# A hybrid attention and SSD layer: the SSD half of the output projection computed by seven products ahead of attention

## The chip, the cores and the metric

The kernel runs on one core of one Trainium2 chip. The metric is device microseconds of one launch, as the median of several runs; lower is better.

## The reference, cut to what matters

One layer, with one sequence of 2048 tokens, a model width of 1024 and float32 everywhere. An input projection feeds two branches of width 1024, attention and an SSD scan. Both are gated and normed, laid side by side and multiplied by one 2048 x 1024 matrix; a residual and a LayerNorm follow.

```python
proj = einsum('bsd,de->bse', x, w_in)                    # 1024 -> 6672 columns
q, k, v, z_att, z_ssm, xbc, dt_raw = split(proj)
y_att = wts[0] * o1 + wts[1] * o2 + wts[2] * o3          # windowed attention, dilations 1, 4, 16
y_att = rms_norm(y_att * silu(z_att), att_norm_g)
...
y = ssd_chunked(xs, dt, a, bm, cm) + d_skip * xs         # chunks of 128 tokens
y_ssm = rms_norm(y * silu(z_ssm), ssm_norm_g)
mix = concatenate([y_att, y_ssm], axis=-1)               # (2048, 2048)
x = layer_norm((2 * DEPTH) ** 0.25 * x + mix @ w_out, ln_g, ln_b)
```

`rms_norm(u, g)` is u / sqrt(mean(u^2) + eps) * g. The factor per token can therefore be applied after the matrix product, and g can be folded into the rows of `w_out`.

## The kernel before, in words

Every float32 product is made of three TensorE (PE) products of split numbers: each operand is a high part (a cast) and a low part (the operand minus its high part), and high x high, high x low and low x high are added in PSUM. A split so costs a cast on ScalarE (ACT) and a subtraction on VectorE (DVE) or GpSimd (POOL).

The kernel has four stretches. Between them and inside them PE, DVE, ACT and POOL run in the order in which the program is written; the order of SyncE's DMAs (SP) is set by a scheduler.

1. The v columns of the projection, with the sums that the second stretch needs.
2. The rest of the input projection, as 44 jobs. A job makes a 256 x 1024 tile of the transposed projection from 2 x 2 blocks by the Strassen-Winograd scheme, which needs seven products in place of eight. A product is 12 matmuls of 128x512 (four slices of the inner dimension, three each), so a job has 84. The token side (`token_side`, seven operands B11, T1, B21, T2, B22, T4, T3, each a high and a low tile of 1 MB) stays for a phase of jobs and is loaded anew where the phase changes, on POOL's queue: phase 0 has 10 jobs, phase 1 has 22, phase 2 has 12. The column side (`column_side`) is built for each job from a raw 256-column piece: ACT casts, POOL subtracts, DVE forms the sums. `products` writes a job; after each of its seven products `flush` adds one to a count, and `after(n, f)` and `later` hang other work on later counts. In this way the 32 SSD units (16 chunks of tokens times 2 groups of channels) run between the products from count 161 on: `spots` says at which count a unit begins, and `ssd1` to `ssd6` are its steps, one a count. `d_us` receives the gated SSD output, and `ssd6` writes a split copy of the first four blocks of 128 tokens to `d_uh`. `wout_load` and `split_w` scale the SSD rows of `w_out` by the norm's gain, split them and store them to `d_wo`, hung on counts 35 to 55.
3. Attention, in 8 pairs of heads. What a pair still needs after its last tile (`statistics`, `gather`, `weights`, `combine`) is a chain of DMAs through DRAM with DVE work between them, written into the program of the next pair. The combined output goes to `d_ua`, and that of pair 7 stays in SBUF (`u7`, tiles named PT). During pair 7 the weights of the SSD half are loaded (`load_w`).
4. The output projection with the norms, for 16 blocks of 128 tokens. Each block has two products of 48 matmuls, `(n, 1)` for the SSD half and `(n, 0)` for the attention half, in the order of `order`: the SSD halves of blocks 0 to 3 first, then their attention halves, and from block 4 on the two halves in turn. The loads of the attention half's weights from `d_wo` are written behind the second product. A half needs `split` (its DVE copy of pair 7 at L994, ACT's cast at L995, the subtraction at L996), `squares` (ACT at L1000, the DVE reduction at L1002), `product` (L1025 to L1027, and at L1031 the matmul that adds up the squares over channels) and `add` (reciprocal at L1039, scaling and adding at L1043). `norm` closes a block: L1049 to L1063 on DVE, then two POOL multiplications and additions with the LayerNorm's vectors (L1064, L1065) and the store.

## Time and profile before

| | |
|---|---|
| median of 3 runs | 2184.16 us (2184.16 to 2184.79) |
| profiled execution, its own time | 2171.41 us |
| span in its profile | 2169.6 us |
| mean clock granted to PE | 0.972 |
| PE busy | 2048.0 us, 94% |
| weight loads (PEld) busy | 1703.7 us, 79% |
| DVE busy | 1394.1 us, 64% |
| ACT busy | 1154.4 us, 53% |
| POOL busy | 1092.5 us, 50% |
| moved by DMA | 525.26 MB, mean 242 GB/s |

The profile is of one execution; its times count from the start of its span. A share of busy time is a mean over the four stretches. The stretches lie at 0 to about 204 us (v), to about 1248 us (projection and SSD), to 1763.5 us (attention) and to 2169.6 us (output). In a list of instructions a row gives start, duration, engine, line, operation, output<-inputs and shape, and in brackets how long the engine stood idle before it and what ended that. A row of waits gives engine, tile and line of the waiting group, what released it, and then the microseconds in all, how often, and the longest.

### The profile page before, as it was taken

How to read it: one execution, taken by the hardware profiler on the slowest of the kernel's cores; microseconds unless marked ns; L12 is line 12 of the kernel's file. 1: busy time of each engine (PE TensorE's matmuls, PEld its weight loads, DVE VectorE, ACT ScalarE, POOL GpSimd, SP SyncE). 2: the span in 40 equal slices, each digit the busy share in tenths (PEclk: the TensorE clock that was granted, in tenths of full speed). 3: DMA queues.
4: the chain of work that ended last, by engine and by line, in shares of the span. 5: the costliest groups of instructions: out<-in, count | busy, mean ns of one | idle time of the engine just before them, and what ended most of it. 6: DMA issues, size and time to landing. Idle time of an engine off the chain costs nothing.

```text
span 2169.6 us, 38851 instructions
## 1 busy us (share of the span) xinstructions
PE 2048.0 (94%) x13824; PEld 1703.7 (79%) x13824; DVE 1394.1 (64%) x3145; ACT 1154.4 (53%) x3007; POOL 1092.5 (50%) x899
## 2 busy tenths in 40 slices
PE   7999998989999999979999999999999977999998
PEld 7998776768887887858888877888878865888886
DVE  3431554548998677835555468888888845655655
ACT  4231444435565677645676468888888841222221
POOL 2122545657886666755555331776666670422222
PEclk9999999989999999999999979999999988999999
DMA  9999778976678888899888853777876799232220
GB/s 330 370 333 338 234 255 281 326 279 213 204 231 293 310 318 302 296 389 298 269 276 286 302 203 88 217 222 220 245 212 185 213 366 286 95 105 84 96 83 29
DMA packets 260801, 525.26 MB, mean 242 GB/s; under 512 B 43712, under 2 KB 122688, under 8 KB 244608
## 3 DMA queue, kind: packets, MB, share of 16 engines
q1 hardware_dynamic: 181984, 255.37, 36.9%
q0 software_dynamic: 35280, 184.30, 24.1%
q10 hardware_dynamic: 43344, 83.12, 11.7%
q8 instruction: 109, 1.79, 0.3%
q14 instruction: 84, 0.69, 0.1%
HBM read 346.15 MB, written 193.33 MB: 249 GB/s over the span
## 4 chain that ended last, share of the span: by engine, by line
PE 47%; DMA 8%; DVE 5%; ACT 3%; issue 3%; POOL 2%; ACTq 0%; SPq 0%; POOLq 0%; DVEq 0%
PE S L816 7%; PE N L865 7%; PE T L845 6%; PE S L1025 4%; PE S L1027 3%; PE S L1026 3%; PE pp L310 3%; PE pp L314 3%; PE pp L312 3%; PE T L1025 2%; PE T L1026 2%; PE T L1027 2%; DMA TT3l<-d_T0T 1%; DVE P L824 1%; ACT P L832 1%
## 5 line engine op out<-in xcount | busy, mean ns | idle before, releaser
L266 POOL TENSOR_TENSOR w<-wr,w 128x512 fp32r<-128x512 f32 x231 | 357.2, 1562 | 177.5 <-ACT w L265 146.5
L832 ACT ACTIVATE P<-P,st 128x256 f32<-128x256 f32 (+1 forms) x768 | 345.1, 451 | 96.6 <-DVE st L824 96.2
L824 DVE CUSTOM_DVE_ANT_0 P<-S,tb 128x256 f32<-128x256 f32 (+1 forms) x768 | 235.4, 362 | 81.3 <-PE S L816 47.2
L319 ACT COPY ev<-pp 128x512 f32<-128x512 f32 x176 | 102.2, 581 | 184.9 <-PE pp L314 123.4
L847 DVE COPY PT<-T 128x512 f32<-128x512 f32 (+1 forms) x304 | 196.5, 677 | 1.3 <-PE T L845 1.3
L845 PE MATMUL T<-ident,P 128*128 128x128 f32 x1200 | 178.8, 286 | 6.0 <-DVE PT L847 6.0
L865 PE MATMUL N<-PT,v 128*64 128x128 f32 x2400 | 176.5, 284 | 0.0
L265 ACT CAST w<-wr 128x512 fp32r<-128x512 f32 x231 | 137.9, 618 | 52.5 <-DVE wr L258 35.8
L865 PEld LDWEIGHTS N<-PT,v 128*64 128x64 f32 x2400 | 129.2, 138 | 33.2 <-issue 22.6
L258 DVE TENSOR_TENSOR wr<-wr 128x512 f32<-128x512 f32 x132 | 145.0, 1099 | 15.6 <-DMA wr<-w 12.5
L845 PEld LDWEIGHTS T<-ident,P 128*128 128x128 f32 x1200 | 129.8, 142 | 30.3 <-DVE PT L847 7.4
L932 POOL TENSOR_TENSOR wb<-num,wb 128x2048 f32<-128x2048 f32 x21 | 96.4, 4591 | 98.1 <-ACT P L832 57.8
L832 ACT ACTIVATION_READ_ACCUMULATOR P<-P,st 128x1 f32 x768 | 143.9, 187 | 0.0
L327 DVE TENSOR_TENSOR ev<-pp,ev 128x512 f32<-128x512 f32 x152 | 100.6, 682 | 53.5 <-PE pp L314 45.2
L816 PE MATMUL S<-kh,qp 64*128 64x256 f32 (+1 forms) x1024 | 126.6, 306 | 0.0
L1002 DVE TENSOR_REDUCE tb<-P 128x128 f32<-128x1024 f32 x32 | 64.0, 2000 | 85.2 <-PE N L1031 49.2
L416 DVE SCALAR_TENSOR_TENSOR acc<-U,cw,acc 128x2048 f32<-128x2048 f32 x36 | 105.2, 2922 | 3.2 <-ACT acc L413 2.8
L816 PEld LDWEIGHTS S<-kh,qp 64*128 64x128 f32 x1024 | 88.9, 188 | 22.0 <-issue 20.9
L367 DVE SCALAR_TENSOR_TENSOR ev<-ev 128x512 f32<-128x512 f32 x64 | 64.2, 1015 | 64.3 <-ACT ev L366 64.2
L150 PE MATMUL pp<-vh,xh 128*128 128x256 f32 (+1 forms) x320 | 90.2, 289 | 15.4 <-ACT xh L173 15.4
L143 POOL TENSOR_TENSOR vl<-vraw,vh 128x256 fp32r<-128x256 f32 (+1 forms) x32 | 29.7, 933 | 130.5 <-ACT vh L142 125.7
L1064 POOL TENSOR_TENSOR kh<-kh,wb 128x1024 f32<-128x1024 f32 x8 | 19.2, 2398 | 142.6 <-DVE kh L1063 142.6
(368 smaller groups left out, 6135.2 us busy)
## 6 DMA issues: line engine op xcount, KB each, us to landing
wr<-w ACTq DMA_DIRECT2D x157, 256.0 KB
v<-d_v POOLq DMA_DIRECT2D x24, 1024.0 KB, 7.0
wb<-d_wd SPq DMA_DIRECT2D x48, 512.0 KB
d_wc<-w SPq DMA_DIRECT2D x44, 512.0 KB
w<-d_wc POOLq DMA_DIRECT2D x44, 512.0 KB, 6.2
csb<-d_cs ACTq DMA_DIRECT2D x32, 512.0 KB
st<-xT SPq DMA_DIRECT2D x31, 512.0 KB
d_v<-vt SPq DMA_DIRECT2D x16, 512.0 KB
```

What stands on the lines that cost most here:

```text
L258: tt = lambda o, a, b, op=OP.subtract: nc.vector.tensor_tensor(q[o], q[a], q[b], op=op)
L265: nc.scalar.copy(t[:, 0], q[nm])
L266: nc.gpsimd.tensor_tensor(t[:, 1], q[nm], t[:, 0].bitcast(F32), op=OP.subtract)
L816: nc.tensor.matmul(ov(sp[h][:, 256 * b:256 * b + w]), A["q"][d][x][hr, blk], kv(A["k"][y][hr]), start=(m == 0), stop=(m == 2))
L824: nc.vector.tensor_tensor_reduce(P[:, h, b, 256 - w:256], sp[h][:, c0:c0 + w], tab[:, h, tab.shape[2] - w:], 1.0, 3.0e38, OP.add, OP.min, ...
L832: nc.scalar.activation(p, p, AF.Exp, bias=stat(A, 0, d, h, blk), scale=-1.0, accum_out=stat(A, 1, d, h, blk))
L845: nc.tensor.transpose(tp[:, h, b], P[:, h, b, 128 * which:128 * which + 128], ident)
L847: nc.vector.tensor_copy(pt[:, :, bl[0]:2], tp[:, :, bl[0]:2])
L865: nc.tensor.matmul(nm[64 * h:64 * h + 64, bq * 128:bq * 128 + 128], v[:, k, 64 * h:64 * h + 64], pts[which][:, h, b], start=(f or not whic ...
L1025: nc.tensor.matmul(ps, uh[:, e, :], wh, start=(e == 0), stop=False)
L1026: nc.tensor.matmul(ps, uh[:, e, :], wl, start=False, stop=False)
L1027: nc.tensor.matmul(ps, ul[:, e, :], wh, start=False, stop=(e == 7))
```

## The change

The SSD half of the output projection leaves the last stretch. It becomes eight more jobs of the second stretch, a phase 3 behind phase 2, each 256 tokens by the 1024 output columns:

- **Token side and column side change places.** Phase 3's resident operands are sums of the blocks of `w_out`'s SSD rows, made by `output_side` at counts 35 to 67 in place of `wout_load`: 16 loads, 16 gains on ACT, 28 casts on ACT, 44 subtractions on DVE, 28 stores of 512 KB on POOL's queue into `d_U`. `output_load` brings them in, two of the seven at count 292 into a pool `op` that takes the place of the SSD's tiles, five during phase 2's last job. The column side comes from `d_us`.
- **The norm of the SSD half.** Each SSD unit gets a square (ACT) and a reduction (DVE) in `ssd6` and a matmul and a small DVE addition in `ssd7`. `rms` makes the factors, `fin_o` scales a job's results and stores them to `d_o`.
- **SSD units stand 4 counts apart** throughout; the first 13 stood 63/13 apart.
- **Attention.** `combine` of pairs 0 to 6 also writes a split copy of blocks 0 to 2 to `d_uh` (a cast and a subtraction on POOL). The DMAs of pair 7's chain are issued by ACT. Pair 6's last step of `combine` moves from the tile (2, 2, 0) to (2, 0, 0). The weights loaded during pair 7 are now those of the attention half.
- **The output stretch** has one product per block. Of blocks 0 to 3 (`F` is 4), `product_early` makes pairs 0 to 6 (42 matmuls) and `keep_early` copies the result to `parts`; `product_last` makes pair 7 (6 matmuls). Then come blocks 4 to 15 whole. The residual is `d_o` plus ALPHA times x, one DVE instruction (`residual_add`). The four norms of blocks 0 to 3 are written in a row.

```diff
-    d_uh = [dtile(f"d_uh{g}", [4, 128, 2, 4, 128]) for g in range(2)]
-    d_wo = dtile("d_wo", [16, 128, 2, D])
+    d_wo = dtile("d_wo", [8, 128, 2, D])
+    d_U = {n: dtile(f"d_U{n}", [2, 128, 4, 512]) for n in ("B11", "B21", "B22", "T1", "T2", "T3", "T4")}
+    d_o = dtile("d_o", [16, 128, D])
+    d_uh = dtile("d_uh", [3, 128, 2, 7, 128])
...
+        def output_side(k, b):
...
+            def item(nm, o, a=None, c=None):
+                def high():
+                    if a:
+                        nc.vector.tensor_tensor(R[o], R[a], R[c], op=OP.subtract)
+                    t = sums.tile([128, 2, 512], F32R, name="wot", bufs=4)
+                    nc.scalar.copy(t[:, 0], R[o])
+                    after(0, lambda: low(t))
+                def low(t):
+                    nc.vector.tensor_tensor(t[:, 1], R[o], t[:, 0].bitcast(F32), op=OP.subtract)
+                    after(1, lambda: nc.gpsimd.dma_start(
+                        dap(d_U[nm], k * 512, [[2048, 128], [128 * 2048, 2], [1, 512]]), t.bitcast(F32)))
...
+            put(b, load)
+            put(b + 1, gain)
+            for n, f in enumerate(items):
+                put(b + 2 + n, f)
...
+        def output_load():
+            def step(i):
+                nm = LEFT[i]
+                T.append([op_.tile([128, 4, 512], F32R, name=f"O{nm}{x}") if i < 2 else
+                          tp.tile([128, 4, 512], F32R, name=f"T{LEFT[i - 2]}{x}") for x in "hl"])
+                for a, t in enumerate(T[-1]):
+                    nc.gpsimd.dma_start(t.rearrange("p k t -> p (k t)"), d_U[nm][a].rearrange("p k t -> p (k t)"))
...
         def ssd6(A):
-            if n < 4:
-                yh, yl = [sd.tile([128, 512], F32R, name=f"xde{p}") for p in "hl"]
...
+            sq = sd.tile([128, 4, 128], F32, name="y")
+            nc.scalar.activation(sq, xd, AF.Square)
+            A["sr"] = sr = sd.tile([128, 128], F32R, name="bsh", bufs=2).bitcast(F32)
+            nc.vector.tensor_reduce(sr, sq.rearrange("p c t -> p t c"), axis=mybir.AxisListType.X, op=OP.add)
+        def ssd7(A):
+            nc.tensor.matmul(pn[:, 0:1], A["sr"], one, start=True, stop=True)
...
+            if g:
+                nc.vector.tensor_tensor(m, m, pn[:, 0:1], op=OP.add)
...
+        def fin_o(i):
+            def f(ci, q, e):
+                n = 2 * i + ci
+                nc.scalar.activation(e, e, AF.Copy, scale=msq[:, n:n + 1])
+                nc.sync.dma_start(d_o[n][:, 512 * q:512 * q + 512], e)
...
+        jobs += [(3, ("o", i)) for i in range(8)]
-        spots = [7 * 23 + 63 * i // 13 if i < 13 else 7 * 32 + 4 * (i - 13) for i in range(32)]
+        spots = [7 * 23 + 4 * i for i in range(32)]
...
-            for j in range(16):
-                later.setdefault(35 + 4 * j // 3, []).append(lambda j=j: wout_load(16 + j))
+            for k in range(4):
+                output_side(k, 35 + 8 * k)
...
+        def chain(A):
+            return nc.scalar if A["pr"] == 7 else nc.sync
...
-                    step = ((1, 0, 0), (1, 1, 0), (1, 3, 0), (2, 2, 0))
+                    step = ((1, 0, 0), (1, 1, 0), (1, 3, 0), (2, 0, 0) if pr == 7 else (2, 2, 0))
...
-            order = [(n, 1) for n in range(4)] + [(n, 0) for n in range(4)]
-            order += [(n, br) for n in range(4, 16) for br in (1, 0)]
...
+            keep = [product_early(0)]
...
+            keep.append(product_early(1))
+            for d in range(3):
+                combine(A, d)
...
+            nc.scalar.copy(e7[:, 0], u7[0])
+            nc.vector.tensor_tensor(e7[:, 1], u7[0], e7[:, 0].bitcast(F32), op=OP.subtract)
+            nc.scalar.activation(q7, u7[0], AF.Square)
...
+            split(4)
+            squares(4)
...
+            for n in range(F):
+                ps = product_last(n)
+                residual_add(n)
+                add(n, *ps)
+                if n == 1:
+                    split(5)
+                    squares(5)
+            for n in range(F):
+                norm(n)
+            for n in range(F, 16):
+                ps = product(n)
+                if F < n < 15:
+                    split(n + 1)
+                    squares(n + 1)
+                residual_load(n)
+                residual_add(n)
+                add(n, *ps)
+                norm(n)
```

**VectorE in the output stretch.** The rows are one block late in the stretch, with the row's number on DVE's list. P is the raw input of a split, num or qp receives its low part, tb1 and tb2 the sums of squares, kh or kl is the block's output row, S and T are PSUM, and wb_22073 holds x. Before, with both halves of the block (the first begins two rows further up, with its split):

```order
2971 L1002 TENSOR_REDUCE tb1_22285<-P_22204 128x128
2972 L1039 RECIPROCAL st_20350<-st_20350 128x1
2973 L1043 SCALAR_TENSOR_TENSOR kh_20351<-T_22224,st_20350,kh_20351 128x512
2974 L1043 SCALAR_TENSOR_TENSOR kh_20351<-T_22251,st_20350,kh_20351 128x512
2975 L996 TENSOR_TENSOR num_20282<-P_22276,num_20282 128x1024
2976 L1002 TENSOR_REDUCE tb1_22348<-P_22276 128x128
2977 L1039 RECIPROCAL st_20350<-st_20350 128x1
2978 L1043 SCALAR_TENSOR_TENSOR kh_20351<-S_22291,st_20350,kh_20351 128x512
2979 L1043 SCALAR_TENSOR_TENSOR kh_20351<-S_22318,st_20350,kh_20351 128x512
2980 L1049 BN_STATS st_20350<-kh_20351 128x6 x2
2981 L1051 BN_AGGR st_20350<-st_20350 128x2
2982 L1054 RECIPROCAL st_20350<-st_20350 128x1
```

After, one block with one half:

```order
3035 L1080 COPY P_22627<-PT_21966 128x128
3036 L1082 TENSOR_TENSOR qp_21824<-P_22627,qp_21824 128x1024
3037 L1088 TENSOR_REDUCE tb1_21822<-P_22627 128x128
3038 L1099 SCALAR_TENSOR_TENSOR kl_21821<-wb_22073,kl_21821 128x1024
3039 L1172 RECIPROCAL st_21819<-st_21819 128x1
3040 L1176 SCALAR_TENSOR_TENSOR kl_21821<-T_22650,st_21819,kl_21821 128x512
3041 L1176 SCALAR_TENSOR_TENSOR kl_21821<-T_22677,st_21819,kl_21821 128x512
3042 L1182 BN_STATS st_21819<-kl_21821 128x6 x2
3043 L1184 BN_AGGR st_21819<-st_21819 128x2
3044 L1187 RECIPROCAL st_21819<-st_21819 128x1
3045 L1196 TENSOR_SCALAR kl_21821<-kl_21821,st_21819 128x1024
```

A block has one split, one reduction, one pair of scalings and one norm on DVE, with the residual's row (L1099) as new; before it had two of each but the norm, and two products of PE beside them.

**GpSimd's queue at the second token-side load.** The rows are POOL's, where phase 1 begins. TB11h to TB21l are the token-side operands, L266 (L313 after) is the column side's subtraction, wot a split piece of `w_out`. Before:

```order
L119 DMA d_wo<-wot 256x1x512
L266 TENSOR_TENSOR w<-wr,w 128x512 x3
L233 DMA TB11h<-d_T1B_116 128x2048
L233 DMA TB11l<-d_T1B_116 128x2048
L266 TENSOR_TENSOR w<-wr,w 128x512 x2
L233 DMA TT1h<-d_T1T_119 128x2048
L233 DMA TT1l<-d_T1T_119 128x2048
L266 TENSOR_TENSOR w<-wr,w 128x512
L233 DMA TB21h<-d_T1B_117 128x2048
L233 DMA TB21l<-d_T1B_117 128x2048
```

After:

```order
L248 DMA d_UB_142<-wot 128x2x512
L268 DMA TB11h<-d_T1B_116 128x2048
L268 DMA TB11l<-d_T1B_116 128x2048
L313 TENSOR_TENSOR w<-wr,w 128x512 x2
L268 DMA TT1h<-d_T1T_119 128x2048
L268 DMA TT1l<-d_T1T_119 128x2048
L248 DMA d_UB_143<-wot 128x2x512
L313 TENSOR_TENSOR w<-wr,w 128x512
L268 DMA TB21h<-d_T1B_117 128x2048
L268 DMA TB21l<-d_T1B_117 128x2048
L248 DMA d_UT_144<-wot 128x2x512
```

The last pieces of `output_side` are stored between the loads of the token side; the last store of `wout_load` stood ahead of them.

**The chain of pair 7.** Before, its DMAs are SP's; the rows are SP's at the end of attention. st and wd are the chain's statistics and weights in DRAM, cm its work tile, wb the weights spread over the partitions.

```order
L893 DMA d_st_151<-sT 16x16x8 x4
L948 DMA d_ua<-wb 128x16x128
L899 DMA cm<-d_st_151 128x6x32
L984 DMA P<-d_us_138 128x512
L984 DMA P<-d_us_139 128x512
L917 DMA d_wd_159<-cm 128x3x32
L930 DMA wb<-d_wd_159 64x2048 x6
```

After, they are ACT's; the rows are ACT's at the same place:

```order
L969 COPY sT<-N 64x128
L977 DMA d_st_158<-sT 16x16x8 x4
L983 DMA cm<-d_st_158 128x6x32
L1087 ACTIVATE P<-P 128x896 x2
L993 ACTIVATE cm<-cm 128x3x32
L1001 DMA d_wd_166<-cm 128x3x32
L1142 COPY qp<-S 128x512 x2
L1081 CAST num<-P 128x896
L1014 DMA wb<-d_wd_166 64x2048 x6
L1087 ACTIVATE P<-P 128x896
```

The chain's DMAs now stand behind ACT's squares of blocks 0 and 1 (L1087) and the copies of the first early product (L1142) instead of behind SP's loads.

324 lines of the change are left out of this document (200 added, 124 removed).

## Prediction

> **What bounds the kernel now.** I read the page first, then busy time by stretch, TensorE's (PE's) waits, and the order of time on PE and VectorE (DVE) in the last stage.
>
> ```profile
> span 2169.6 us, 38851 instructions
> PE   7999998989999999979999999999999977999998
> DVE  3431554548998677835555468888888845655655
> ...
> 425.00:470.00 45.00, 33.64 (x117) 24.88 (x116) 9.44 (x14) 9.99 (x16) 19.48 (x25) 0.85 0.96 360
> 470.00:530.00 60.00, 59.72 (x264) 48.95 (x263) 52.02 (x39) 34.71 (x56) 44.45 (x32) 1.00 0.57 176
> 750.00:900.00 150.00, 145.47 (x796) 120.29 (x796) 115.89 (x166) 106.48 (x214) 103.91 (x78) 1.00 0.85 304
> 1763.50:1850.00 86.50, 59.69 (x234) 47.43 (x234) 37.55 (x41) 15.82 (x22) 17.90 (x23) 0.84 0.94 291
> 1850.00:2160.00 310.00, 310.00 (x1367) 252.38 (x1366) 180.54 (x225) 74.76 (x106) 84.31 (x30) 1.00 0.25 84
> ...
> PE N L1031 <- DVE tb L1002: 19.8, 3, 14.7
> PE S L1025 <- DMA num<-d_uh: 7.0, 1, 7.0
> ```
>
> A window row gives start:end, length, then busy time (instructions) of PE, PEld, DVE, ACT, POOL, then granted clock, DMA share and GB/s. PE is the bound nearly everywhere: 310.00 of 310.00 from 1850 to 2160. Its two weak places that the change touches are the load of a new token side (425 to 470: 117 matmuls where 60 us later 264 run in 60 us) and the joint between attention and output (1763.5 to 1850), where 26.8 us are idle and the clock falls to 0.84. DVE is at 180.54 of 310 in the last stage and at 115.89 of 150 while SSD runs. The sum is made against the profiled execution (span 2169.6, run 2171.41); the median of the runs is 2184.16, 12.75 us above it, and I carry differences over unchanged.
>
> **The last stage as it is.** The rows are PE, then DVE and POOL, in order of time.
>
> ```profile
> 1229.30 0.39 PE L310 MATMUL pp<-TB11h,w 128*128 128x512 f32 x1
> 1232.02 0.39 PE L310 MATMUL pp<-TT1h,w 128*128 128x512 f32 x1
> ...
> 1770.61 0.79 PE L1025 MATMUL S<-kh,num 128*128 128x512 f32 x1 [7.05 <-DMA num<-d_uh]
> 1836.96 0.28 PE L1031 MATMUL N<-one,tb 128*128 128x1 f32 x2
> 1848.31 0.28 PE L1031 MATMUL N<-one,tb 128*128 128x1 f32 x2
> ...
> 2001.85 0.75 DVE L1043 SCALAR_TENSOR_TENSOR kh<-T,st,kh 128x512 f32<-128x512 f32 x1 [2.79 <-PE T L1027]
> 2002.52 1.28 DVE L1049 BATCH_NORM_STATS2 st<-kh 128x6 f32<-128x512 f32 x2
> 2003.83 0.21 DVE L1051 BATCH_NORM_AGGREGATE st<-st 128x2 f32<-128x12 f32 x1
> 2004.40 0.16 DVE L1054 RECIPROCAL st<-st 128x1 f32<-128x1 f32 x1 [0.36 <-ACT st L1053]
> 2004.60 0.81 DVE L1063 TENSOR_SCALAR kh<-kh,st 128x1024 f32<-128x1024 f32 x1
> 2005.33 0.22 DVE L994 COPY P<-PT 128x128 f32<-128x128 f32 x1
> 2006.67 2.31 DVE L996 TENSOR_TENSOR num<-P,num 128x1024 fp32r<-128x1024 f32 x1 [1.12 <-ACT num L995]
> 2010.10 2.04 DVE L1002 TENSOR_REDUCE tb<-P 128x128 f32<-128x1024 f32 x1 [1.13 <-ACT P L1000]
> 2012.05 0.16 DVE L1039 RECIPROCAL st<-st 128x1 f32<-128x1 f32 x1
> 2012.25 0.75 DVE L1043 SCALAR_TENSOR_TENSOR kh<-S,st,kh 128x512 f32<-128x512 f32 x1
> ...
> 2005.49 2.40 POOL L1064 TENSOR_TENSOR kh<-kh,wb 128x1024 f32<-128x1024 f32 x1 [17.07 <-DVE kh L1063]
> 2007.97 3.28 POOL L1065 TENSOR_TENSOR kh<-kh,wb 128x1024 f32<-128x1024 f32 x1
> ...
> L996 DVE TENSOR_TENSOR qp<-P,qp x9: 1215/1226/2308, 1845.0 to 2120.1; 128x1024 fp32r<-128x1024 f32 x9
> L367 DVE SCALAR_TENSOR_TENSOR ev<-ev x64: 678/698/1785, 638.9 to 1234.0; 128x512 f32<-128x512 f32 x64
> ...
> 2160.78 0.75 DVE L1043 SCALAR_TENSOR_TENSOR kl<-S,st,kl 128x512 f32<-128x512 f32 x1 [4.36 <-PE S L1027]
> ```
>
> A product of 48 matmuls (one block, one half) takes 1848.31 - 1836.96 = 11.35 us, 0.2335 a matmul with the N matmul's 0.14 taken off. Twelve matmuls of the projection take 1232.02 - 1229.30 = 2.72 us, 0.2267 each. DVE works in program order, and it stands still 1.12 us for ACT's cast and 1.13 for ACT's squares in each split.
>
> **Removed from the last stage.** Sixteen products with their N matmuls, 16 x 11.35 = 181.6 us of PE.
>
> **Added to the projection.** Eight jobs of 84 matmuls, 672 x 0.2267 = 152.4 us of PE, on the path since PE has no room there. The 32 matmuls of ssd7 add 32 x 0.14 = 4.5. Together +156.9. Beside these 19 us a job has 7 casts, 3 keeps and 4 scalings on ACT, 7 subtractions on POOL, and 4 sums and 4 additions on DVE, which is the load of any job now without SSD; they are hidden by PE. The d_o stores go to SP, which has nothing behind them that PE waits for.
>
> **The last stage after.** PE starts at 1770.6, as now: the first input stands at the same place of POOL's queue. Four early products have 4 x 42 = 168 matmuls, 39.2 us, and 2.6 more for the slow clock after the gap: done at 1812.4. Their last matmuls need pair 6 of d_uh; combine 3 of pair 6 comes earlier than now for that, and I cost it at nothing (bounds 0 and 4 us).
>
> Then pair 7 is needed.
>
> ```profile
> 1800.94 2.29 DVE L932 TENSOR_TENSOR wb<-num,wb 128x2048 f32<-128x2048 f32 x1 [2.08 <-DMA wb<-d_wd]
> ...
> 1817.07 2.29 DVE L932 TENSOR_TENSOR wb<-num,wb 128x2048 f32<-128x2048 f32 x1 [3.39 <-DMA wb<-d_wd]
> 1819.39 2.50 DVE L937 TENSOR_TENSOR PT<-wb 128x512 f32<-128x512 f32 x4
> ...
> num<-d_wo POOLq DMA_DIRECT2D x4, 1024.0 KB, 12.0
> ```
>
> Now its combine ends at 1821.9, its loads of weights 8 us apart because d_wo comes in beside them. Those d_wo loads are gone, but ACT issues the chain behind squares and one PSUM copy. I take the combine 7 us earlier, 1814.8 (bounds 1809 and 1822), and the split of pair 7 for four blocks done at 1817.2 after a reduction.
>
> From here DVE has, in one row: a reduction 1.75; split and reduction of block 4, 5.6 (copy 0.22, waits 1.12 + 1.13, subtraction 1.2, reduction 1.95); for each of four blocks the residual 1.2 (128x1024 from SBUF, twice L367's 0.698 less one start), two PSUM additions 1.25, a reciprocal 0.2, two scalings 1.25, so 4 x 3.9 = 15.6; split and reduction of block 5, 5.6; four norms of 2002.52 to 2005.33, 4 x 2.8 = 11.2; block 4 itself 5.5. That is 45.3. The norms stand in a row for the first time, so POOL's L1064 and L1065 of one run beside the next: between 0 (the 0.81 of L1063 above) and six instructions at 2.31 - 1.22 = 1.1, 6.6; I take 3. So 1865.5 before block 6 is split, while PE needs for the same 24 + 96 matmuls only some 30 us, to 1848: PE idles.
>
> The Trainium skill, SBUF — State Buffer, Who interferes with whom, says that DVE and GpSimd hold their shared SBUF port as an exclusive lock for a whole instruction. The trace agrees: L996, begun at 2006.67, ends 1.1 us after L1064 does, and L1065 is longer by as much. By it each of the four norms and the residual after them would wait for POOL's instruction to end, 6 us in place of my 3.
>
> For blocks 6 to 15 one round of DVE is 2012.05 - 2005.33 = 6.72 (copy to reduction, waits included), residual 1.2, reciprocal 0.2, first addition 0.67, and 2005.33 - 2001.85 = 3.48 (second addition to the end of L1063): 12.25 us, above PE's 11.35. With 2.31 and 1.22 in turn for L996 it is still 11.7. Ten rounds are 122.5: 1988. The last product ends 2.8 us into DVE's last round, and from the last addition to the end it is 2169.6 - 2160.8 = 8.8: 1999.6. So the stage ends 170.0 earlier. If DVE kept up it would end at 1967.6 (1815.4, then 24 matmuls, then 12 x 11.35, then 9.2), 202 earlier; with the combine as late as now it is 163.
>
> **The weights of the SSD half and the second token side.**
>
> ```profile
> DMA to landing us min/median/max: 3.6/6.5/10.6
> ACT wot L117 <- DMA d_wo<-wot: 5.3, 2, 3.7
> PE pp L310 <- ACT ev L319: 24.4, 10, 7.6
> PE pp L312 <- DMA TB21l<-d_T1B: 3.3, 1, 3.3
> ```
>
> In place of 16 gains and 16 stores of 512 KB there are 16 gains, 28 casts, 44 subtractions on DVE and 28 stores, 6.3 MB more. The last seven stores (3.7 MB) now stand between the loads of the second token side on POOL's queue. At the 360 GB/s of 425 to 470 they are 10 us of transfer there, where PE already waits for every second operand. ACT waits for a store to land before it can cast again (5.3 us now), and PE waits for ACT behind it (24.4 over all). Bounds -3 (the old waits gone, the new ones hidden) and 25 (10, and four times 4 for the raw loads, which are used one step after their issue); I take 11, near the transfer.
>
> **SSD closer together.** The first 13 units stand 4 steps apart instead of 63/13 = 4.85, and each has a square (ACT 0.6), a reduction of 128x512 (DVE, half of 2.04) and a small addition, 1.2 us of DVE.
>
> ```profile
> DVE ev L367 <- ACT ev L366: 11.8, 7, 3.1
> DVE mt L539 <- ACT mt L535: 8.4, 6, 2.3
> ```
>
> DVE is at 77% there (115.89 of 150), and these waits for ACT are most of the rest. With 1.2 us more in a unit's 17 it is at 84%; scaled by 4.85/4 at over 100%. PE loses 4.5 of 150 now. Bounds -3 and 24; I take 8, a third, since the reduction falls into a wait for ACT. From 1000 on DVE has room.
>
> **The rest.** The third token side: two of seven operand pairs come early into a pool of their own, the other five (10.5 MB, 29 us at 360 GB/s) begin as the last job's first product ends and are due 24 to 35 us later: 0 to 5, I take 1. On POOL a cast and a subtraction per pair (about 1.5 us in 62) lie in its idle time: 0 to 3, I take 1.
>
> **Sum**: -170.0 + 156.9 + 11 + 8 + 2 = +7.9, a span of 2177.5 and 2192 for the runs.
>
> **Rivals.**
> DVE keeps up in the last stage: then it ends at 1967.6 and the sum is -24, 2160. The point is whether DVE's 48 us before block 6 and its 12.25 a round fit into PE's 30 and 11.35. For it speaks only DVE's 58% now; against it stands the row of rounds above. This ends on the other side.
> The projection swallows its extra work: the two terms of 11 and 8 are nothing, -11, 2173. For it: before 425 ACT and DVE are not full, and stores and SSD work may fall into waits that exist. This too is faster.
> DVE leads in the SSD stage too, with the token side late in full (24 and 25): +38, 2222.
> The products do not run ahead, because their token side comes late: decided by whether 10.5 MB land in 35 us; at half the rate PE would wait 25 us, 2216.
>
> **Chances.** The sum as it stands, 2183 to 2203: 0.40. DVE keeping up: 0.12. The projection swallowing: 0.26. The slow projection: 0.15. The late token side: 0.04; others 0.03. A measurement tells 0.2%, 4.4 us, from no change. Faster than 2179.8: 0.12 + 0.22 + 0.02 = 0.36. Within: 0.12 of the first and 0.04 of the third, 0.16. Slower: 0.28 + 0.19 + 0.01 = 0.48. The range of 8 in 10 reaches into the faster and the slower cases, 2162 to 2214; that of the likeliest alone is 2183 to 2203.
>
> **What would show it.** From the split of pair 7 on, DVE should be at over 85% and PE should wait for DVE's subtraction at the start of nearly every product, once for some 15 us; products should be 12 us apart. If they are 11.4 apart, the term of the last stage is wrong. A wait of PE for token operands of over 20 us in the second load, and one for mt or ev in SSD, would show those terms; a full PE row in both makes the second rival right. Eight jobs of 19 us without a wait must stand ahead of attention.

## The result, and the profile after

The changed kernel is slower: 2263.44 us, the median of 4 runs (2259.55 to 2270.01), against 2184.16 us before. The ratio is 1.0366, with a 95% interval of 1.0338 to 1.0393. Forecast were 2192 us with a range of 2162 to 2214 us; the time lies 49 us above its upper end.

The profiled execution took 2259.55 us, with a span of 2257.7 us, 88.1 us more than the span before. The medians lie 79.3 us apart, since the execution profiled before was 12.8 us faster than its median and this one only 3.9 us. The page's first line and PE's row of busy tenths, 56 us a slice:

```profile
span 2257.7 us, 39253 instructions
...
PE   7999896869999999988999989989999999988698
```

PE's weak slices are now the seventh to the ninth (339 to 508 us, at 6, 8 and 6) and the fifth to third from the end (8, 8 and 6). From 740 to 1330 us, with the SSD units, no slice stands out: what is lost there is spread. Busy time by stretch (start:end, length, PE, PEld, DVE, ACT, POOL, then clock, DMA share, GB/s): the end of phase 0 with the second load of a token side, a piece of the SSD stretch, the eight new jobs, and the output stretch in two pieces.

```profile
353.40:510.50 157.10, 115.09 (x422) 87.79 (x422) 71.38 (x84) 57.32 (x102) 83.64 (x89) 0.86 0.83 297
800.00:950.00 150.00, 142.29 (x800) 116.53 (x800) 112.56 (x177) 111.36 (x224) 100.70 (x76) 1.00 0.75 263
1330.50:1492.00 161.50, 157.10 (x673) 127.42 (x671) 47.40 (x60) 64.96 (x115) 71.21 (x57) 0.98 0.46 167
2011.80:2110.00 98.20, 76.53 (x315) 61.14 (x311) 57.06 (x72) 18.40 (x32) 17.95 (x11) 0.90 0.67 202
2110.00:2250.00 140.00, 118.49 (x500) 93.50 (x500) 107.97 (x137) 26.20 (x44) 74.08 (x28) 0.93 0.43 155
```

The first row is the worst: 42 of 157 us of PE idle, and the clock at 0.86. The stretch before with the same matmuls:

```profile
343.00:467.00 124.00, 105.45 (x423) 83.15 (x422) 52.49 (x60) 47.07 (x81) 70.33 (x77) 0.92 0.93 328
```

There 18.6 us were idle. So of the 33 us more, 23 are PE standing and 10 are the same matmuls taking longer, at a granted clock of 0.86 in place of 0.92. The SSD row has DVE at 75%, far from full. In the last row PE is idle for 21.5 of 140 us, and DVE has 108.

To place the 88 us, each trace is cut where PE's work shows a joint: the first matmul of job 0, of job 11 (so that the first job of phase 1, which waits for the token side, still counts to phase 0) and of job 22, the end of job 43, the first and the last matmul of attention. Lengths in us, one profiled execution each; the names are the beginnings of those of the runs below.

| run | v | phase 0 | phase 1 | SSD | eight jobs | attention | output | span | ratio to before (95%) |
|---|---|---|---|---|---|---|---|---|---|
| before | 209.4 | 257.3 | 212.3 | 569.5 | | 514.9 | 406.3 | 2169.6 | |
| after | 210.7 | 299.7 | 213.1 | 607.1 | 161.3 | 520.1 | 245.6 | 2257.7 | 1.0366 (1.0338 to 1.0393) |
| e1 | 210.8 | 275.8 | 215.3 | 614.1 | 162.3 | 519.4 | 245.1 | 2242.8 | 1.0278 (1.0262 to 1.0295) |
| e2 | 210.2 | 302.8 | 218.5 | 606.4 | 162.9 | 519.4 | 243.3 | 2263.6 | 1.0400 (1.0379 to 1.0420) |
| e3 | 210.4 | 254.6 | 214.5 | 592.1 | | 515.1 | 409.4 | 2196.0 | 1.0074 (1.0056 to 1.0092) |
| e4 | 211.1 | 302.6 | 213.4 | 611.0 | 163.1 | 518.4 | 235.7 | 2255.2 | 1.0333 (1.0284 to 1.0382) |
| e5 | 211.7 | 302.5 | 218.8 | 582.5 | 173.6 | 526.9 | 247.1 | 2263.0 | 1.0358 (1.0337 to 1.0379) |
| e6 | 209.0 | 302.2 | 217.8 | 586.5 | 161.6 | 519.7 | 245.9 | 2242.6 | 1.0284 (1.0254 to 1.0314) |
| e7 | 212.5 | 300.6 | 220.6 | 609.4 | 167.1 | 525.1 | 224.8 | 2260.1 | 1.0303 (1.0285 to 1.0320) |
| e8 | 211.4 | 269.2 | 220.0 | 606.9 | 160.2 | 518.1 | 245.4 | 2231.3 | 1.0223 (1.0199 to 1.0247) |
| v1 | 211.7 | 270.6 | 213.7 | 573.9 | 181.5 | 525.1 | 223.8 | 2200.4 | 1.0070 (1.0050 to 1.0090) |
| v2 | 210.7 | 269.2 | 217.4 | 572.4 | 180.6 | 535.0 | 220.0 | 2205.4 | 1.0108 (1.0067 to 1.0149) |
| v3 | 210.7 | 267.6 | 219.2 | 582.0 | 175.8 | 538.8 | 212.5 | 2206.7 | 1.0106 (1.0087 to 1.0125) |
| v4 | 211.2 | 268.7 | 215.3 | 583.5 | 170.6 | 524.7 | 239.3 | 2213.2 | 1.0162 (1.0132 to 1.0192) |

Phase 1 is the same code in the first ten runs and still lies between 212 and 221 us: a difference under 8 us in one stretch of one profile proves nothing by itself.

So the output stretch gives back 160.7 us and the eight jobs cost 161.3 us: they cancel. The loss is what the prediction had as two small terms: phase 0 (42.4 us) and the SSD stretch (37.6 us), with 5.2 us in attention and 2.1 us before and between.

The waits of the changed kernel, longest in total first (engine, tile and line that waited, what released it: us in all, times, longest). For PE:

```profile
PE pp L357 <- ACT ev L366: 39.6, 11, 9.7
PE ss L651 <- DVE bsh L646: 31.3, 17, 3.6
PE S L1117 <- ACT num L1081: 17.6, 1, 17.6
...
PE S L1117 <- DMA num<-d_uh: 13.6, 2, 9.1
```

PE's wait for ACT's copies has grown from 24.4 to 39.6 us, the second row did not exist, and the third is the one long wait for a split that was forecast at some 15 us. What ACT waited for between 320 and 510 us, in the same view:

```profile
ACT woraw L236 <- DMA woraw<-wout: 28.9, 6, 9.8
ACT wot L243 <- DVE woraw L241: 22.9, 10, 4.1
ACT wot L243 <- DMA d_UB<-wot: 17.9, 3, 9.0
```

And one such wait, ACT in order of time (start, duration, engine, line, operation):

```profile
366.70 0.56 ACT L366 COPY ev<-pp 128x512 f32<-128x512 f32 x1
366.96 0.45 ACTq L232 DMA_DIRECT2D woraw<-wout  x1
...
370.70 0.72 ACT L236 ACTIVATE woraw<-woraw,gc 128x512 f32<-128x512 f32 x1
381.21 0.72 ACT L236 ACTIVATE woraw<-woraw,gc 128x512 f32<-128x512 f32 x1 [9.79 <-DMA woraw<-wout]
...
383.57 0.57 ACT L366 COPY ev<-pp 128x512 f32<-128x512 f32 x1
```

with PE behind it:

```profile
384.19 0.80 PE L357 MATMUL pp<-TT3h,w 128*128 128x512 f32 x1 [9.69 <-ACT ev L366]
```

The four raw pieces are loaded on ACT's queue at 366.96 and scaled one step later. ACT stands 9.79 us for their landing, the copy that PE needs stands behind it, and PE waits 9.69 us.

### The profile page after: what moved, and what is told of

Its sections match the earlier page's. It is cut to its first block, busy times and chain, and to the rows that moved or that the text cites. A ratio compares the mean times of both kernels' runs of the same rounds, so it can differ in the third digit from the quotient of the medians.

```text
span 2257.7 us, 39253 instructions
## 1 busy us (share of the span) xinstructions
PE 2066.3 (92%) x13768; PEld 1708.4 (76%) x13768; DVE 1438.5 (64%) x3235; ACT 1204.7 (53%) x3128; POOL 1188.7 (53%) x978
## 4 chain that ended last, share of the span: by engine, by line
PE 34%; DMA 10%; DVE 9%; ACT 8%; issue 4%; POOL 2%; ACTq 1%; SPq 0%; DVEq 0%; POOLq 0%
PE S L896 5%; PE N L945 5%; PE T L925 5%; PE pp L357 5%; PE pp L359 5%; PE pp L361 5%; DMA zt<-d_zs 3%; ACT P L912 2%; ACT mt L578 1%; DVE P L904 1%; DMA TB22l<-d_UT 1%; DMA d_kl<-ev 1%; PE ss L618 1%; DMA kl<-d_kl 1%; DMA w<-d_wc 1%
## 5 line engine op out<-in xcount | busy, mean ns | idle before, releaser
L313 POOL TENSOR_TENSOR w<-wr,w 128x512 fp32r<-128x512 f32 x287 | 437.5, 1540 | 284.6 <-ACT w L312 212.4
L366 ACT COPY ev<-pp 128x512 f32<-128x512 f32 x208 | 121.1, 582 | 288.4 <-PE pp L361 188.7
L374 DVE TENSOR_TENSOR ev<-pp,ev 128x512 f32<-128x512 f32 x184 | 122.1, 684 | 167.4 <-PE pp L361 101.1
L305 DVE TENSOR_TENSOR wr<-wr 128x512 f32<-128x512 f32 x164 | 173.2, 1056 | 35.7 <-DMA wr<-w 24.7
L312 ACT CAST w<-wr 128x512 fp32r<-128x512 f32 x287 | 171.2, 618 | 38.4 <-DVE wr L305 23.2
L414 DVE SCALAR_TENSOR_TENSOR ev<-ev 128x512 f32<-128x512 f32 x64 | 69.1, 1093 | 65.1 <-ACT ev L413 65.1
L896 PEld LDWEIGHTS S<-kh,qp 64*128 64x128 f32 x1024 | 88.9, 188 | 22.1 <-issue 20.4
L357 PE MATMUL pp<-TT3h,w 128*128 128x512 f32 x176 | 77.1, 438 | 29.8 <-ACT ev L366 29.6
L357 PE MATMUL pp<-TB22h,w 128*128 128x512 f32 x208 | 87.1, 419 | 10.5 <-ACT ev L366 6.1
```

The costliest lines, as they stand in the source:

```text
L305: tt = lambda o, a, b, op=OP.subtract: nc.vector.tensor_tensor(q[o], q[a], q[b], op=op)
L312: nc.scalar.copy(t[:, 0], q[nm])
L313: nc.gpsimd.tensor_tensor(t[:, 1], q[nm], t[:, 0].bitcast(F32), op=OP.subtract)
L357: nc.tensor.matmul(ps, w[:, 0, k], th[:, k], start=start and k == 0, stop=False, skip_group_check=not start)
L366: nc.scalar.copy(e, ps)
L374: nc.vector.tensor_tensor(e, a, e, op=op)
```

## The experiments

Twelve kernels were run. The first eight change one place of the changed kernel, but for e3, which changes one of the kernel before.

**e1: raw weights three steps earlier.**

```diff
-                    R[nm] = sums.tile([128, 512], F32, name="woraw", bufs=4)
+                    R[nm] = sums.tile([128, 512], F32, name="woraw", bufs=6)
...
-            put(b, load)
-            put(b + 1, gain)
+            put(b, lambda: load(("B12", 0, 1), ("B11", 0, 0)))
+            put(b + 2, lambda: load(("B21", 1, 0)))
+            put(b + 3, lambda: load(("B22", 1, 1)))
+            put(b + 3, lambda: gain(("B11", 0), ("B12", 0)))
+            put(b + 5, lambda: gain(("B21", 1)))
+            put(b + 6, lambda: gain(("B22", 1)))
...
-                output_side(k, 35 + 8 * k)
+                output_side(k, 35 + 7 * k)
```

> Of the changed kernel, with the raw pieces of the SSD weights loaded three steps ahead of their gain (six buffers in place of four, the operands in another order) and everything else as it is. Theory: ScalarE stands behind the landing of raw pieces (28.9 us in six waits between 320 and 510 us) and TensorE behind ScalarE's copies, which makes most of the 43 us lost up to phase 1. Then the time falls by 20 to 30 us, to about 2235 to 2243, and the waits of ScalarE for woraw nearly vanish. Rival: the stores to d_U and the traffic beside the token side are the cost; then it falls by less than 8 us, with the wait moved to wot or to the operands' loads.

The edit also gives the raw pieces six buffers, puts the operands in another order and the four groups seven counts apart instead of eight.

2241.79 us. Phase 0 falls by 23.9 us, from 299.7 to 275.8, and the wait of 28.9 us is 3.7 us:

```profile
ACT wot L243 <- DVE woraw L241: 16.8, 9, 4.6
...
ACT woraw L236 <- DMA woraw<-wout: 3.7, 2, 3.5
```

The theory holds: over half of phase 0's loss was ACT behind its own loads. PE's wait for ACT's copies falls with it, from 39.6 to 27.2 us.

**e8: subtractions and stores out of ACT's way as well.**

```diff
             def low(n, t):
                 nm, o = items[n][:2]
                 nc.vector.tensor_tensor(t[:, 1], R[o], t[:, 0].bitcast(F32), op=OP.subtract)
+                if n < 6 and len(items[n + 1]) > 2:
+                    o, x, y = items[n + 1][1:]
+                    nc.vector.tensor_tensor(R[o], R[x], R[y], op=OP.subtract)
-                after(1, lambda: nc.gpsimd.dma_start(
+                after(0, lambda: nc.sync.dma_start(
```

> Of the changed kernel, with the raw pieces loaded three steps ahead as in the run e1_loads_early, each subtraction of blocks one step ahead of its cast, and the stores to d_U on SyncE right behind the low part instead of a step later on GpSimd. Theory: of the 18 us by which phase 0 is still longer than before in that run, ScalarE's waits for VectorE's subtraction (16.8 us) and for the stores of wot (19.0 us) are the cause; phase 0 falls from 275.8 us to 260 to 267 us and the time to about 2227 to 2235. Rival: the extra 6.3 MB beside the second token side are the cause, which no order removes: phase 0 stays above 271 us.

2233.45 us; phase 0 takes 269.2 us, 6.6 less than in e1. It ends 2 us above the theory's interval. The rest is at the load of the token side (window rows as above, e8 first, then before):

```profile
425.00:480.60 55.60, 39.15 (x123) 28.36 (x122) 15.09 (x21) 11.90 (x22) 27.56 (x35) 0.82 1.03 393
```

```profile
425.00:467.00 42.00, 30.64 (x104) 22.40 (x103) 6.44 (x12) 9.52 (x15) 17.63 (x23) 0.84 1.01 380
```

In both, the DMA engines are full (shares of 1.03 and 1.01), and e8 moves 5.9 MB more at nearly the same rate. Job 10, which waits for the operands, takes 46.7 us in e8 and 37.8 us before, 8.9 us more. That is the extra traffic beside the load, and close to the 10 us that the prediction had for it; it is the rival's cause, with about half of the 18 us that it was meant to explain.

**e2: the matmul of the squares two counts later.**

```diff
-                for d, f in ((0, ssd1), (1, ssd2), (2, ssd3), (3, ssd4), (4, ssd5), (5, ssd6), (6, ssd7)):
+                for d, f in ((0, ssd1), (1, ssd2), (2, ssd3), (3, ssd4), (4, ssd5), (5, ssd6), (8, ssd7)):
-            after(n0 + 7, out_plan)
+            after(n0 + 9, out_plan)
```

> Of the changed kernel, with ssd7 (the matmul that adds up the squares) two counts later and everything else as it is. Theory: TensorE stands at that matmul for VectorE's reduction, which is written one step ahead of it (31.3 us in 17 waits); two steps later the reduction is done, and the time falls by 20 to 30 us, to about 2233 to 2243. Rival: VectorE or ScalarE is the bound of the SSD stretch with units four counts apart; then TensorE waits as long at another place (mt, ev, xs), and the time falls by less than 8 us.

2266.72 us: nothing won, and the SSD stretch is 606.4 us against 607.1. The theory falls. The 31.3 us went to other places; two of the rows that took over:

```profile
PE ss L569 <- DVE msq L656: 10.7, 5, 2.9
PE ss L569 <- DVE msq L654: 8.3, 4, 3.1
```

These are the next unit's transposes, waiting for the PSUM bank that DVE's small addition to msq has to free. The pool ss has three banks, and ssd7 is one more user.

**e3: the spacing alone, in the kernel before.**

```diff
-        spots = [7 * 23 + 63 * i // 13 if i < 13 else 7 * 32 + 4 * (i - 13) for i in range(32)]
+        spots = [7 * 23 + 4 * i for i in range(32)]
```

> Of the kernel before, with the SSD units four counts apart throughout and nothing else changed. Theory: the closer spacing alone costs 0 to 5 us, 2184 to 2189, since the 38 us of the SSD stretch are the new matmul's waits. Rival: the density is the cost, and this is 15 to 25 us slower, 2199 to 2209.

2197.14 us against 2179.86 us for the kernel before measured beside it, a ratio of 1.0074. The rival holds: the SSD stretch grows by 22.6 us, without any new work. PE's wait for mt grows from 4.9 to 10.6 us:

```profile
PE ss L570 <- DVE mt L539: 10.6, 7, 3.2
```

Jobs 24 to 30 take 1 to 6 us more each. DVE's busy share is not higher there (108.6 of 150 us from 750 to 900, against 115.9 before), so the cost lies in steps that wait for each other, not in a full engine. Over the whole SSD stretch PE is idle for 39.5 us against 26.5 before; the other 9.6 us are the same matmuls taking longer (552.5 against 543.0 us busy), at a granted clock of 0.97 in place of 0.99.

**e5: the old spacing, in the changed kernel.** The edit is that of e3 the other way, with the loads of the last five operand pairs three counts later.

> Of the changed kernel, with the SSD units at the spacing of the kernel before (the first 13 stand 63/13 counts apart) and so the loads of the third token side three counts later; squares, reduction and matmul per unit stay. Theory now: the spacing is the larger part of the SSD stretch's loss (alone, in the kernel before, it made that stretch 22.6 us longer, 569.5 to 592.1); then the stretch falls from 607 us to 580 to 590 us, the first of the eight jobs is 3 to 8 us later, and the time falls by 12 to 22 us, to about 2241 to 2251. Rival: the extra squares fill VectorE at either spacing; then the stretch stays above 600 us and the time falls by less than 5 us.

2261.63 us. The SSD stretch falls by 24.6 us to 582.5, as expected, yet the time does not: the eight jobs take 173.6 us (12.3 more: in the first of them PE waits 10.4 us for operands, against 4.4), attention 526.9 us (6.8 more, about half of it at its start), and phase 1 5.7 more, which is within the scatter named above. The denser spacing buys the early load of the third token side. Undoing it gives about as much back as it takes.

**e6: squares in the eight jobs.** `ssd6` and `ssd7` are gone; `column_side` of the new jobs squares and sums the raw blocks that it has loaded.

```diff
+            def square(nm):
+                t = op_.tile([128, 4, 128], F32, name="sq", bufs=1)
+                nc.scalar.activation(t, q[nm], AF.Square)
+                sr[nm] = op_.tile([128, 128], F32, name="sr", bufs=4)
+                nc.vector.tensor_reduce(sr[nm], t.rearrange("p c t -> p t c"), axis=mybir.AxisListType.X, op=OP.add)
```

> Of the changed kernel, with the squares, the reductions and the matmuls that add them up taken out of the SSD units and done in the eight new jobs from the blocks loaded there; the spacing stays at four counts. Theory: they are the smaller part of the SSD stretch's loss; it falls from 607 us to 588 to 596 us, near the 592.1 of the kernel before at this spacing, the eight jobs stay at 161 to 165 us, and the time falls by 10 to 18 us, to about 2245 to 2253. Rival: with the spacing gone close, nothing is won by taking the squares out: less than 5 us.

2247.04 us. The SSD stretch falls by 20.6 us to 586.5, and the eight jobs stay at 161.6 us, though not job by job: the first is 5.4 us shorter, the others 1 us longer each. The theory holds. Spacing and squares share the 37.6 us about evenly (24.6 and 20.6 by undoing each, 45.2 together, which is the sum within the scatter).

**e4: no x in the output stretch**, so that one DVE instruction of 1.2 us a block is missing.

```diff
                 ps = product_last(n)
-                residual_add(n)
...
-                residual_add(n)
                 if n + 2 < 16:
                     input_load(n + 2)
```

> Of the changed kernel, without the 16 instructions that add the scaled input x in the output stretch (the input is left out of the sum there). Theory: VectorE is the bound of that stretch, with 12.2 us a block against 11.35 us for the matmuls; without 1.2 us a block the blocks come 11.4 us apart, and with the four first ones the time falls by 12 to 17 us, to about 2247 to 2251. Rival: something else sets the distance of the blocks (loads, the clock); then it falls by less than 4 us.

2254.12 us; the output stretch falls by 9.9 us, 2 us short of the theory's lower end. The intervals of the two ratios to the kernel before overlap, so the time alone would not show the gain; the distance of the blocks does. The distance of the blocks is read from PE's N matmul, one a block. Late in the changed kernel, and then in e4:

```profile
2169.27 0.28 PE L1123 MATMUL N<-one,tb 128*128 128x1 f32 x2
2181.50 0.28 PE L1123 MATMUL N<-one,tb 128*128 128x1 f32 x2
```

```profile
2149.80 0.28 PE L1123 MATMUL N<-one,tb 128*128 128x1 f32 x2
2161.14 0.28 PE L1123 MATMUL N<-one,tb 128*128 128x1 f32 x2
```

Blocks 9 to 15 come (2242.7 - 2169.3) / 6 = 12.23 us apart in the changed kernel, and 11.3 to 11.4 in e4. With 1.2 us less on DVE, PE is the bound.

**e7: DVE's order in the output stretch.** x is added in the eight jobs, splits run two blocks ahead, and the norms of blocks 0 to 3 are spread.

```diff
+                nc.vector.scalar_tensor_tensor(e, xa[:, 2 * ci + q], ALPHA, e, op0=OP.mult, op1=OP.add)
                 nc.sync.dma_start(d_o[n][:, 512 * q:512 * q + 512], e)
...
             for n in range(F, 16):
                 ps = product(n)
-                residual_add(n)
+                if n + 2 < 16:
+                    split(n + 2)
                 add(n, *ps)
+                if n + 2 < 16:
+                    squares(n + 2)
                 norm(n)
+                if n < 2 * F:
+                    norm(n - F)
```

> Of the changed kernel, with the output stretch relieved on VectorE: the scaled input is added in the eight new jobs instead (VectorE is at 30% there), splits run two blocks ahead, and the norms of blocks 0 to 3 stand one each behind those of blocks 4 to 7. Nothing is left out. Theory: VectorE's order alone makes TensorE wait 17.6 us before block 6 and sets 12.2 us a block; then all blocks come 11.4 us apart without that wait, and the stretch falls from 245.6 us to 212 to 222 us, the time to about 2230 to 2240. The eight jobs get at most 3 us longer. Rival: the products wait for something else there (the loads, or the combine of pair 7); then the stretch falls by less than 12 us.

2250.98 us. The output stretch falls by 20.8 us to 224.8, 3 us above the theory's upper end; the wait of 17.6 us is gone, and blocks come 11.3 to 11.4 us apart, but for two at 13.2 and 16.4 where DVE still has the early norms. The time falls by less than the theory's 23 to 33 us, since the eight jobs take 5.8 us more, twice the allowance, and attention 5.0. It starts late in the changed kernel too, and this run pointed to the reason. SP in the changed kernel, in order of time:

```profile
1471.99 23.15 SPq L666 DMA_DIRECT2D d_o<-ev  x7
1495.24 1.53 SPq L838 DMA_DIRECT2D tb<-tabs  x3
```

Attention's first table, tb, is loaded behind the last stores of d_o, and DVE's first instruction there waits for it. Attention's eighth tile starts 3.6 us later, counted from its first matmul, than before. In e7 those stores wait for DVE as well, and it is 9.4 us (in v1, with the same stores, 3.2: the size varies).

**v1: all four edits.**

> The changed kernel with all four edits together: weights pipelined (as e8), squares in the eight jobs (as e6), the SSD units at the old spacing (as e5; the first two operand pairs are loaded at count 301), the output stretch relieved (as e7). Theory: the gains lie in different stretches and add up. Phase 0 near 269 us, the SSD stretch 565 to 575 us, the eight jobs 170 to 178 us (later operands), attention 519 to 527 us, the output stretch near 225 us: a span of about 2172 to 2190 us, the time within 1% of the kernel before on either side. Rival: the edits stand in each other's way (the eight jobs carry squares, input loads and late operands at once, so they take over 185 us), and the time stays above 2205 us.

2195.09 us, 0.7% above the kernel before, within the theory's 1%; the span, 2200.4 us, lies 10 us above its interval. By the ratios (1.0366 and 1.0070) four fifths of the loss are won back by order and place alone, in the stretches that were named. The eight jobs are the exception, at 181.5 us: the first takes 39.9 us in place of 27.1, where squares, loads of x and late operands meet (PE waits 11.7 us for operands), and the others 20.4 in place of 19.2.

**v2: the joints.** Pair 6's split copy stays in SBUF, the loads for the first early product stand at (1, 2, 1) instead of (1, 3, 0), and the last job's stores go to POOL's queue.

> The kernel of the run v1_all_mended with three edits at the joints: the split copy of pair 6 stays in SBUF for the early products instead of going through DRAM (its two stores took 11.5 us to issue and ran beside those of pair 7's chain, which took 12.5 us against 2.1 us before); the loads for the first early product stand two tiles earlier on GpSimd's queue; the last job's stores of d_o leave SyncE's queue, behind which the attention table of pair 0 was issued, and the norm's factors lie in a buffer that attention does not take over. Theory: the output stretch falls by 6 to 14 us against v1 and attention by 3 to 6 us, the time by 8 to 18 us. Rival: the chain of pair 7 is as long without the collision, since its own small stores are what is slow; then the output stretch falls by less than 4 us.

2204.18 us. The output stretch gains 3.8 us and attention loses 9.9: the rival holds. Attention does not lose them at its start, where its eighth tile is 1.8 us late against 3.2 in v1; later PE waits 10.8 us in six waits for loads of kl, a low part of the keys (4.1 us in v1). Why these come later is not shown. From the first to the last of the chain's four small stores ACT's queue still takes 8.84 us, in order of time:

```profile
1987.47 8.84 ACTq L985 DMA_DIRECT2D d_st<-sT  x4
```

They took 2.14 us on SP before and 12.49 us on ACT in the changed kernel:

```profile
1764.15 2.14 SPq L893 DMA_DIRECT2D d_st<-sT  x4
```

```profile
2017.40 12.49 ACTq L977 DMA_DIRECT2D d_st<-sT  x4
```

The combine of pair 7 ends 53.3 us after attention, as in the changed kernel (53.4); before it was 58.6. A single one of these issues takes 0.31 to 0.35 us on ACT's queue and 0.32 to 0.72 on SP's; what is long on ACT is the standing between them, 9.1 us before the third in the changed kernel. What ends it the profile does not name, and the cause stays open.

**v3: DVE's order once more,** with casts three blocks ahead, the early norms behind every second block, six gaps of five counts in the SSD spacing, and the last stores on ACT's queue.

> The kernel of the run v2_joint with the last job's stores of d_o on ScalarE's queue (on GpSimd's they stood ahead of attention's first loads, and attention took 535.0 us against 525.1), with the SSD units between the two spacings (six gaps of five counts, then four, so that the first two operand pairs are loaded five counts earlier), and with VectorE's order in the output stretch made once more: casts three blocks ahead, the norms of blocks 0 to 3 behind every second block, the squares of block 2 ahead of the chain's last part. Theory: attention is back at 517 to 522 us, the SSD stretch and the eight jobs together fall from 753 us to 743 to 750 us, and the output stretch from 220 us to 206 to 213 us, since blocks 8 and 9 no longer come 13 and 16 us apart: a time of 2168 to 2184 us, near that of the kernel before (2178). Rival: the gains in the output stretch are eaten by the start, where TensorE waits for the first operands and the chain; then it stays above 216 us and the time above 2186 us.

2206.58 us. The output stretch, 212.5 us, is as expected: every block 11.3 to 11.4 us apart. The SSD stretch and the eight jobs together are 757.8 us, not 743 to 750, and attention takes 538.8 us. DVE and POOL at the start of attention, in order of time:

```profile
1459.28 8.09 DVE L674 SCALAR_TENSOR_TENSOR ev<-TT4l,ev 128x512 f32<-128x512 f32 x1 [1.16 <-ACT ev L673]
```

```profile
1459.52 2.30 POOL L868 CAST qp<-qh 128x512 fp32r<-128x512 f32 x4
1461.75 2.28 POOL L868 CAST qp<-ql 128x512 fp32r<-128x512 f32 x4
1463.98 2.28 POOL L872 CAST qp<-qh 128x512 fp32r<-128x512 f32 x4
1466.21 2.73 POOL L872 CAST qp<-ql 128x512 fp32r<-128x512 f32 x4
```

The last addition of x takes 8.09 us instead of 0.7, and ends only when 13 of POOL's 16 casts in a row have run, and during the 14th. PE's first tiles of attention wait 7.9 us for DVE behind it.

**v4: each stretch as it was shortest,** with x added by DVE in the output stretch for blocks 4 to 15.

> Each stretch as it was shortest so far: weights pipelined (e8), SSD units four counts apart with the squares in the eight jobs (e6), x added in the projection for blocks 0 to 3 alone and by VectorE in the output stretch for the others, the output stretch ordered as in v3_ordered, pair 6's split copy in SBUF, the last job's stores on ScalarE's queue, and the loads for the first early product back at their old tile. Theory: in v3_ordered the last addition of x ran beside GpSimd's permuting casts and took 8.1 us in place of 1.1, which made attention start 9.0 us late, and the loads moved ahead cost 7 us at the start of pair 7's last dilation; without both, attention takes 515 to 521 us, the SSD stretch and the eight jobs 745 to 752 us, the output stretch 211 to 219 us: a time of 2175 to 2190 us, not clear of the kernel before. What stays is 10 us of phase 0 and some 20 us in which the eight jobs' operands and the SSD units are late, more than the 25 us that the seven products can save. Rival: VectorE is again the bound of the output stretch with x added there; then blocks come over 11.8 us apart and it takes over 222 us.

2213.97 us. Attention's tiles now start as they did before (0.2 us earlier at the eighth, against 3.6 later in the changed kernel): with the d_o stores off SP's queue and no addition of x beside POOL's casts, that term is gone. It loses 9.8 us all the same, at later places, and ends above the theory: PE waits 8.7 us in four waits for loads of kl, against 1.1 us before. And the output stretch is back at 239.3 us, as the rival said: the last blocks come 13.1 or 15.9 us apart, DVE is busy for 61.4 of the 68 us from 2124 to 2192, and PE waits for its reduction. Adding x, 1.22 us in the changed kernel, takes up to 3.42 here, beside POOL's additions:

```profile
2150.05 0.38 PE L1141 MATMUL N<-one,tb 128*128 128x1 f32 x2 [1.35 <-DVE tb L1104]
2159.06 3.42 DVE L1117 SCALAR_TENSOR_TENSOR kh<-num,kh 128x1024 f32<-128x1024 f32 x1
2165.94 0.38 PE L1141 MATMUL N<-one,tb 128*128 128x1 f32 x2 [1.37 <-DVE tb L1104]
```

No version beats the kernel before. The nearest, v1, is 0.5 to 0.9% slower.

## Why the prediction was wrong

By its own terms, from the profiles (the eight jobs with the third operand load):

| term | predicted | bounds given | measured |
|---|---|---|---|
| output stretch | -170.0 | -202 to -163 | -160.7 |
| eight jobs, third token side | +152.4, +1 | 0 to 5 on the second | +161.3 |
| weights and second token side | +11 | -3 to 25 | +42.4 |
| ssd7 and SSD closer together | +4.5, +8 | -3 to 24 on the second | +37.6 |
| attention, and the rest | +1 | 0 to 3 | +7.3 |
| sum | +7.9 | | +87.9 |

**Output stretch: right in mechanism, 9 us short,** and 2 us outside its bounds. The rounds of DVE were worked out at 12.25 us and measured 12.23; PE's one long wait was put at some 15 us and was 17.6. One sign that was named does not show: DVE is busy for 77% of the time there, not over 85%, since a round holds its waits for ACT. Here is one round, DVE in order of time:

```profile
2135.15 0.81 DVE L1196 TENSOR_SCALAR kh<-kh,st 128x1024 f32<-128x1024 f32 x1
2135.88 0.22 DVE L1080 COPY P<-PT 128x128 f32<-128x128 f32 x1
2137.21 2.31 DVE L1082 TENSOR_TENSOR num<-P,num 128x1024 fp32r<-128x1024 f32 x1 [1.12 <-ACT num L1081]
2140.65 2.00 DVE L1088 TENSOR_REDUCE tb<-P 128x128 f32<-128x1024 f32 x1 [1.13 <-ACT P L1087]
2142.56 1.22 DVE L1099 SCALAR_TENSOR_TENSOR kl<-wb,kl 128x1024 f32<-128x1024 f32 x1
...
2147.36 0.81 DVE L1196 TENSOR_SCALAR kl<-kl,st 128x1024 f32<-128x1024 f32 x1
```

That is the row of instructions that the sum was made of, 12.2 us from L1196 to L1196, and e4, e7 and v3 show that it is the bound. What was missed is small and stands ahead of block 6: pair 6's copy was late by 4.4 us (taken as 0, bounds 0 and 4), the combine came 2 us later than taken, and block 4's row of d_o was waited for, 2.9 us. DVE beside POOL's L1197 and L1198, taken at 3 us, cost 5.3, as the rows behind the four norms show (a 128x1024 of L1099 takes 1.22 alone, L1196 0.81, L1080 0.22, L1082 1.23):

```profile
2114.00 2.70 DVE L1099 SCALAR_TENSOR_TENSOR kh<-wb,kh 128x1024 f32<-128x1024 f32 x1 [2.88 <-DMA kh<-d_o]
...
2120.28 1.47 DVE L1196 TENSOR_SCALAR kh<-kh,st 128x1024 f32<-128x1024 f32 x1
2121.68 2.36 DVE L1080 COPY P<-PT 128x128 f32<-128x128 f32 x1
2125.14 2.21 DVE L1082 TENSOR_TENSOR num<-P,num 128x1024 fp32r<-128x1024 f32 x1 [1.11 <-ACT num L1081]
```

The prediction's estimate by the rule of the Trainium skill (SBUF — State Buffer, Who interferes with whom), 6 us, is nearer in size than the 3 taken, but in part by luck: it had each of the four norms wait for POOL, and their L1196 took 0.81, 1.10, 0.81 and 0.81 us. The loss fell on the rows behind them.

**Eight jobs: right in count, 8 us short.** Seven of them stand 19.2 us apart. The first takes 27.1, with waits of 0.7, 2.4 and 1.3 us for its operands, at a granted clock of 0.87. That is the late third token side, taken as 1 us. The prediction also said of the d_o stores that SP has nothing behind them that PE waits for. It had attention's first table, and v4, where the last job's stores leave SP, shows those 3.6 us gone.

**Weights: the step that failed most.** The prediction sized the stores' traffic (10 us) and the waits that it saw in the kernel before. It named ACT behind a landing and PE behind ACT, but priced the raw loads at four times 4 us, and only in the upper bound. They were 28.9 us in six waits. The subtraction written one instruction ahead of its cast, another 22.9 us of ACT's standing, was not priced at all: the working listed 44 subtractions on DVE and did not ask who stands behind them. From PE's side the 42.4 us are 15 us more of waiting for ACT's copies (18.6 to 33.8 us), 4 for ACT's casts of the column side, 9 for the token operands (11.2 to 20.5 us), and 14 in which the same matmuls take longer, at a granted clock of 0.88 in place of 0.93. Of this lower clock, which came with the waits, the term had nothing. e1 and e8 take back 30.5 of the 42.4 us by order, buffers and the choice of queue; about 9 are the traffic.

**SSD stretch: wrong in what decides.** The working asked whether DVE would be full (84%, or over 100%) and took 8 us, a third of its upper bound of 24. DVE was not full, 75%. The cost was in the order: with units closer together each job there has more steps that wait for another engine (e3, 22.6 us with no new work), and the squares lengthen that chain by some 20 us (e6). The whole stretch, before and after:

```profile
679.00:1248.50 569.50, 542.96 (x2917) 447.25 (x2915) 346.56 (x549) 363.33 (x731) 330.05 (x288) 0.99 0.88 305
```

```profile
723.60:1330.50 606.90, 561.96 (x2979) 459.02 (x2978) 374.60 (x610) 380.14 (x763) 338.36 (x303) 0.97 0.84 288
```

PE is idle for 18 us more and busy for 19 more. Of the 19, some 8 are the matmuls of ssd7, 0.24 us for each unit and not 0.14; the lower clock has a part in the rest. As for the reduction falling into a wait for ACT, DVE's waits in the stretch, before and then after, say that it did:

```profile
DVE mt L539 <- ACT mt L535: 46.7, 21, 9.3
```

```profile
DVE bsh L646 <- ACT y L644: 34.4, 18, 4.4
...
DVE mt L587 <- ACT mt L583: 12.0, 10, 6.2
```

DVE stands as long for ACT as before, 46.4 us against 46.7. But most of it is now at the reduction, and PE stands behind that for 31.3 us, where it stood 4.9 us behind mt. The working asked whether DVE had the time, and not who waits for DVE at that place.

**Rivals.** The one called slow projection, 2222 us, came nearest in place: the same two terms at 24 and 25 us. Its reason for the first, DVE leading, is not what the rows show. The rival in which the products come late for want of their operands had 25 us; it was 8. That DVE keeps up, and that the projection swallows the work, are refuted by the rows above.

What stays open: which of the waits between ACT and DVE makes the closer spacing cost 22.6 us, since none of the edits changes one alone (DVE's wait for ACT's copies ev grows from 62.9 to 88.7 us in e3, that for mt falls from 46.7 to 32.3); and whether a fuller rework could profit from the idea. It removes 181.6 us of matmuls and adds 156.9, so the matmuls alone win 25 us. The order of the output stretch can add to that: in v3 the stretch is 193.8 us shorter than before. The losses left in v1 to v4 are larger than the two together.
